# Moving matmul operands to other 64-byte quarters of a 256-byte line in a one-layer conformer and SwiGLU block

## The chip, the core and the metric

The kernel runs on one core of a Trainium2 chip. The metric is the device time of one execution in microseconds (us). TensorE multiplies (PE in the rows; PEld is its load of the stationary operand), VectorE is DVE, ScalarE is ACT, GpSimd is POOL, and SyncE (SP) issues the weight transfers. TensorE's granted clock was 1.00 of full speed, the 2.4 GHz level, in nearly the whole run.

## The reference, cut to what matters

One layer on 272 tokens (16 meta tokens and 256 real ones) with 2048 channels:

```
u = rms_norm(h, g1)
a, g = split(u @ w_in + b_in)               # 2048 x 4096
u = depthwise_conv31(a * sigmoid(g)) + b_dw
u = silu(layer_norm(u)) @ w_out + b_out     # 2048 x 2048
h = h + rms_norm(u, g2)
u = rms_norm(h, g3)
u = (silu(u @ w_gate) * (u @ w_up)) @ w_down  # 2048 x 5632 twice, 5632 x 2048
return (h + rms_norm(u, g4))[16:]
```

## The kernel before

**Split precision.** Every large product is made from fp32r operands in two parts: a high part (the value rounded) and a low part (the rest). ACT casts a raw fp32 weight block to its high part (L155), DVE or POOL subtracts to get the low part (L157). A product is high by high, high by low and low by high.

**Stages, in order.** "in" has 16 groups of two weight tiles; a step in depth is three matmuls of 272 columns (L218 to L220) with a weight part as the stationary operand and an activation part streaming: high weights by high activations, high weights by low activations, low weights by high activations. "out" and "gate/up" hold the high and low activations of a step side by side, so that a step is a pair: L227 streams 512 columns past the high weights, L228 streams 256 columns past the low weights (in the last out group, L223 does it in three matmuls of 256). There are 240 pairs in out and 1408 in gate/up, which has 22 groups of 4 weight tiles. "down" turns the roles round: 128 tokens of the SwiGLU result (tile `hid`) are stationary, and 512 columns of down weights stream past them, in threes (L773 to L775): high by high, high by low, low by high. There are 352 threes in down and 512 in in.

**Weight flow.** `PLAN` lists 360 blocks of at most 128 x 1024; `prep` fetches, casts and subtracts a block, up to three blocks ahead of TensorE. The order on PE, ACT, DVE and POOL is the order in which the code is written.

**Where operands start.** A partition's bytes can be counted in lines of 256 bytes (`LINE`, 64 values) and quarters of 64 bytes (16 values). In the built program every tile `hi`, `lo`, `hid` and `moving` begins at a multiple of 256. A weight tile of 128 columns is 512 bytes, so all tiles of a block begin at one quarter. The activations begin at quarter 0, but the low activations of in, which follow 272 columns of high ones, begin at quarter 1. The low weights of in, out and gate/up are put half a line in (`LO_AT` is 32 values), at quarter 2; all else begins at quarter 0.

The identity matrix `ident` (two POOL instructions) is made first of all; it is used for the convolution's diagonals and one matmul at the end of in.

Of the kernel before, what the change touches and what calls it, by code (L numbers as in the profile page):

```python
# [8 lines left out]
F32 = mybir.dt.float32  # L9
F32R = mybir.dt.float32r  # L10
# [3 lines left out]
P = 128  # L14
D = 2048
F = 5632
SEQ = 256
# [5 lines left out]
NF = F // P  # L23
RMS_EPS = 1e-6
LN_EPS = 1e-5
SB = 1024
# [15 lines left out]
def plan():  # L42
    out = []
    for name, groups, n_k in (
        ("in", IN_GROUPS, NK),
        ("out", OUT_GROUPS, NK),
        ("gu", FFN_GROUPS, NK),
        ("down", DOWN_GROUPS, NF),
    ):
        for g, tiles in enumerate(groups):  # L50
            n = len(tiles) * (2 if name == "gu" else 1)
            for k, kb in sub_blocks(n, n_k):
                out.append((name, g, n, k, kb))
    return out


PLAN = plan()
# [1 line left out]


LINE = 64
LO_AT = 32
MOVE = 2 * L + 32
LOOK = 3
RAW = 4

# [10 lines left out]
HID_LATE = 4  # L77
# [5 lines left out]
def conformer_swiglu_kernel(ctx: ExitStack, tc: tile.TileContext, xT, wflat, vec, w_dw, gain, out):  # L83
    nc = tc.nc
# [4 lines left out]
    const = ctx.enter_context(tc.tile_pool(name="const", bufs=1))  # L89
    wp = ctx.enter_context(tc.tile_pool(name="wp", bufs=4))  # L90
# [3 lines left out]
    def bank():  # L94
        return mm.tile([P, 512], F32, tag="bank", name="bank")
# [5 lines left out]
    def moving(cols, nm):  # L101

        t = xs.tile([P, NK, MOVE], F32R, tag="moving", name=nm)
        return t[:, :, :cols]
# [15 lines left out]
    last_sq = const.tile([P, SEQ], F32, name="last_sq")  # L120
    ones = const.tile([P, P], F32, name="ones")
    nc.gpsimd.memset(ones, 1.0 / D)
    ident = const.tile([P, P], F32, name="ident")
    make_identity(nc, ident)


    offs, off = [], 0
# [7 lines left out]
    def load(i):  # L135
        if i >= len(PLAN) or i in raws:
            return
        _, _, n, _, kb = PLAN[i]
        sz = n * kb * P
        raw = wp.tile([P, SB], F32, tag="raw", name="raw", bufs=RAW)  # L140
        nc.sync.dma_start(
            out=raw[:, :sz], in_=wflat[offs[i] : offs[i] + P * sz].rearrange("(p f) -> p f", p=P)
        )
        raws[i] = raw

    def prep(i):
        name, _, n, _, kb = PLAN[i]
        sz = n * kb * P
        for j in range(i, i + RAW):
            load(j)  # L150
        raw = raws.pop(i)
        hi = wp.tile([P, SB], F32R, tag="hi", name="hi")
        at = 0 if name == "down" else LO_AT
        lo = wp.tile([P, SB + LINE], F32R, tag="lo", name="lo")[:, at : at + SB]
        nc.scalar.copy(out=hi[:, :sz], in_=raw[:, :sz])  # L155
        eng = nc.gpsimd if i < FIRST["out"] + 10 or 0 <= i - FIRST["gu"] < 10 else nc.vector
        eng.tensor_tensor(  # L157
            out=lo[:, :sz], in0=raw[:, :sz], in1=hi[:, :sz].bitcast(F32), op=ALU.subtract
        )
        ready[i] = (hi, lo)  # L160

    def ahead(i, n):

        while n and state["next"] <= min(i + LOOK, len(PLAN) - 1) and state["next"] < state["cap"]:
            prep(state["next"])
            state["next"] += 1
            n -= 1

    def table(func):

        t = small.tile([P, 1], F32, tag="table", name="table")
        nc.scalar.activation(out=t, in_=ones[:, 0:1], func=func)
# [5 lines left out]
    def in_stages(tasks, start=0):  # L178
        for k, t in enumerate(tasks):
            for j, f in enumerate(t):  # L180
                while len(pending) <= start + k + j:
                    pending.append([])
                pending[start + k + j].append((-j, f))
# [6 lines left out]
    def matmuls(name, g, banks, moving, n_k, before=None, step=None, one_half=False, at={}):  # L190

        s_no = 0
        for i, (nm, gg, n, k0, kb) in enumerate(PLAN):
# [3 lines left out]
            if step and s_no:  # L197
                ahead(i, LOOK + 1)
            if step:
# [4 lines left out]
            else:  # L204
                ahead(i, LOOK + 1)
            hi, lo = ready.pop(i)
# [27 lines left out]
    def rsqrt(r, src, eps, n, between=None, first=None, fill=()):  # L234

        y = small.tile([P, L], F32, tag="rs_y", name="rs_y", bufs=1)
        nc.scalar.activation(out=y[:, :n], in_=src, func=AF.Abs_reciprocal_sqrt, bias=eps)  # L240
        m = small.tile([P, L], F32, tag="rs_m", name="rs_m", bufs=1)
        nc.scalar.mul(out=m[:, :n], in_=y[:, :n], mul=-0.5)
        if between:
            between()
        a = small.tile([P, L], F32, tag="rs_a", name="rs_a", bufs=1)
        nc.vector.tensor_tensor(out=a[:, :n], in0=y[:, :n], in1=y[:, :n], op=ALU.mult)
        if first:
            fy = last_sq
            nc.vector.scalar_tensor_tensor(
                out=fy[:, :n], in0=first[1], scalar=-0.5, in1=y[:, :n], op0=ALU.mult, op1=ALU.mult  # L250
            )
        nc.vector.scalar_tensor_tensor(out=a[:, :n], in0=src, scalar=eps, in1=a[:, :n], op0=ALU.add, op1=ALU.mult)
        for f in fill:
            f()
        if first:
            nc.vector.scalar_tensor_tensor(
                out=first[0], in0=a[:, :n], scalar=-3.0, in1=fy[:, :n], op0=ALU.add, op1=ALU.mult
            )
        nc.vector.scalar_tensor_tensor(out=r, in0=a[:, :n], scalar=-3.0, in1=m[:, :n], op0=ALU.add, op1=ALU.mult)
# [32 lines left out]
    xh, xl = x_mv[:, :, :L], x_mv[:, :, L:]  # L292
    front = tc.tile_pool(name="front", bufs=1)
    fr = front.__enter__()
    tp = ctx.enter_context(ExitStack())
    tmp = tp.enter_context(tc.tile_pool(name="tmp", bufs=2))
    done = {"x": 0, "ln": 0, "h": 0}
# [148 lines left out]
    def step(c, s, banks):  # L446
# [3 lines left out]
        if s == 0 and p >= 0:  # L450
            def behind_gate():
                ahead(4 * c, LOOK + 1)
                if c - 3 >= UNSHIFTED:
                    square(c - 3)
# [52 lines left out]
    b = conv(last, *glu_banks[last], lambda: None)  # L507
# [38 lines left out]
    def less_mean(c):  # L546
        lns[c] = zz[:, c, :SEQ]
        nc.vector.tensor_tensor(out=lns[c], in0=lns[c], in1=mean, op=ALU.subtract)

    def silu(c):  # L550
# [11 lines left out]
        rln, var, LN_EPS, SEQ, between=lambda: table(AF.Silu), first=(lns[0], lns[0]), fill=[lambda: less_mean(2)]  # L562
# [18 lines left out]
    acc = const.tile([P, SEQ], F32, name="acc")  # L581
# [27 lines left out]
    for g, tiles in enumerate(OUT_GROUPS):  # L609
        banks = [bank() for _ in tiles]  # L610
        end = g == len(OUT_GROUPS) - 1
        if end:
# [3 lines left out]
            at={NK - 5: drain, NK - 2: sum_of_squares} if end else {},  # L616
# [48 lines left out]


    r2 = const.tile([P, SEQ], F32, name="r2")
    acc2 = const.tile([P, SEQ], F32, name="acc2")
    cell = {}

    def add_squares(q):
# [7 lines left out]
    def factor():  # L679
        st = bank()  # L680
        nc.tensor.matmul(st[:, :SEQ], lhsT=ones, rhs=acc2, start=True, stop=True)
        rsqrt(r2, st[:, :SEQ], RMS_EPS, SEQ)

        sqs.__exit__(None, None, None)
        back = ctx.enter_context(tc.tile_pool(name="back1", bufs=1))
        cell["hids"].append(back.tile([P, HID_LATE, 2 * SEQ], F32R, name="hid1"))

    def hid(f, s):
        late = f >= NF - HID_LATE
        return cell["hids"][late][:, f - (NF - HID_LATE if late else 0), s]  # L690

    def swiglu(f, pg, pu):
        tb, ts = cell["tb"], []
# [25 lines left out]
    for g, tiles in enumerate(FFN_GROUPS):  # L719
        banks = [bank() for _ in range(4)]  # L720
        matmuls("gu", g, banks, h_mv, NK, before=residual if g == 0 else None)
        if g == 0:
            tp.close()
            front.__exit__(None, None, None)
            back = ctx.enter_context(tc.tile_pool(name="back0", bufs=1))
            cell["hids"] = [back.tile([P, NF - HID_LATE, 2 * SEQ], F32R, name="hid0")]
            cell["tb"] = ctx.enter_context(tc.tile_pool(name="tb", bufs=2))
            sqs = tc.tile_pool(name="sqs", bufs=2)
            cell["sqp"] = sqs.__enter__()
        tasks = [swiglu(f, banks[i], banks[2 + i]) for i, f in enumerate(tiles)]  # L730
        if g == 0:
            in_stages([[t[0]] for t in tasks])
            in_stages([[lambda q=q: add_squares(q)] for q in range(4)] + [[factor]])
            in_stages([t[1:] for t in tasks], start=5)
        else:
            in_stages([(lambda t=t: (t[0](), t[1]()), t[2], t[3]) for t in tasks])

    free = xs.tile([P, NK * MOVE], F32, tag="moving", name="free")
    tr = free[:, : NK * SEQ].rearrange("p (c t) -> p c t", c=NK)
# [102 lines left out]
    for g in range(len(DOWN_GROUPS)):  # L842
# [4 lines left out]
        late = mine[-LAG:] if g == len(DOWN_GROUPS) - 1 else []  # L847
        for i in mine:
            ahead(i, LOOK + 1)
            down(i, bs, (0,) if i in late else (0, 1))  # L850
# [67 lines left out]
```

## Time and profile before

| what | value |
|---|---|
| timed runs | 1063.78, 1067.93, 1068.65 us; median 1067.93 |
| profiled execution, its own time | 1064.57 us |
| its span, first to last instruction | 1062.8 us |
| PE busy, PEld busy | 99 %, 88 % of the span |
| granted TensorE clock, mean | 0.997 |

The span is what the rows below divide up; 1.8 us of the profiled execution's time lie around it. Busy time of PE says little, because a matmul's record runs on while the next one has begun (a record of 392 ns, a next start 229 ns later); the distance from start to start is what a matmul costs. The three timed runs lie 4.9 us apart.

### The profile page before, as it was taken

To read this page: it belongs to the slowest core of one execution; us is meant where nothing else is said; L and a number is where in the kernel's file an instruction comes from. 1 tells how busy PE (TensorE), PEld (TensorE's weight loads), DVE (VectorE), ACT (ScalarE), POOL (GpSimd) and SP (SyncE) were. 2 spreads that over 40 slices of the span, in tenths; PEclk is the share of its full clock that TensorE was granted. 3 is DMA by queue.
4 is the path that set the end of the run, shared out by engine and by line. 5 is a ranking of instruction groups with operands and counts; after the bars stand their busy time and mean duration, and the time that the engine had idled before them with its cause. 6 is when DMAs were issued, how large, how long until landed. Compare 5 with 4: busy or idle time off the path is not lost.

```text
span 1062.8 us, 16372 instructions
## 1 busy us (share of the span) xinstructions
PE 1048.7 (99%) x6142; PEld 932.2 (88%) x6142; DVE 692.4 (65%) x1193; ACT 584.3 (55%) x918; POOL 321.2 (30%) x191
## 2 busy tenths in 40 slices
PE   9999999999999999999999999999999999999996
PEld 8999999988888888888888888888888888888885
DVE  5699999987447866555666556665666635454544
ACT  6877877767567655444554445444454334343432
POOL 5889999955245111111111111111111000000000
PEclk9999999999999999999999999999999999999998
DMA  7555656527664666666666666666666896667662
GB/s 254 175 169 174 178 173 171 170 65 211 187 177 124 214 195 186 193 188 190 194 184 195 185 193 191 188 194 185 195 186 191 214 269 215 194 195 192 191 195 97
DMA packets 71841, 197.62 MB, mean 186 GB/s; under 512 B 22993, under 2 KB 24529, under 8 KB 71633
## 3 DMA queue, kind: packets, MB, share of 16 engines
q1 hardware_dynamic: 61728, 192.90, 61.6%
q10 hardware_dynamic: 10032, 3.67, 1.4%
q8 instruction: 48, 0.79, 0.3%
q14 instruction: 33, 0.26, 0.1%
HBM read 192.35 MB, written 2.10 MB: 183 GB/s over the span
## 4 chain that ended last, share of the span: by engine, by line
PE 96%; DVE 1%; DMA 1%; ACT 1%; issue 0%; SPq 0%; POOL 0%; DVEq 0%; ACTq 0%; POOLq 0%
PE bank L227 36%; PE bank L228 18%; PE bank L773 8%; PE bank L774 8%; PE bank L775 8%; PE bank L219 6%; PE bank L220 6%; PE bank L218 6%; DMA raw<-wflat 1%; PE bank L414 1%; PE bank L223 1%; ACT hi L155 0%; SPq L107 0%; POOL lo L157 0%; DVE x_mv L311 0%
## 5 line engine op out<-in xcount | busy, mean ns | idle before, releaser
L155 ACT CAST hi<-raw 128x1024 fp32r<-128x1024 f32 x360 | 377.8, 1050 | 418.1 <-PE bank L227 185.2
L157 DVE TENSOR_TENSOR lo<-raw,hi 128x1024 fp32r<-128x1024 f32 x276 | 341.1, 1236 | 315.7 <-ACT hi L155 315.6
L227 PE MATMUL bank<-h_mv,hi 128*128 128x512 f32 x1408 | 488.9, 392 | 1.2 <-DVE h_mv L645 1.2
L228 PE MATMUL bank<-h_mv,lo 128*128 128x256 f32 x1408 | 395.4, 281 | 0.0
L227 PEld LDWEIGHTS bank<-h_mv,hi 128*128 128x128 f32 x1408 | 264.3, 188 | 59.7 <-issue 1.3
L228 PEld LDWEIGHTS bank<-h_mv,lo 128*128 128x128 f32 x1408 | 264.7, 188 | 0.0
L157 POOL TENSOR_TENSOR lo<-raw,hi 128x1024 fp32r<-128x1024 f32 x84 | 201.2, 2405 | 49.4 <-ACT hi L155 47.9
L715 POOL TENSOR_TENSOR hid<-sw_s,hid 128x256 fp32r<-128x256 f32 x44 | 64.9, 1476 | 412.5 <-ACT hid L714 412.5
L218 PE MATMUL bank<-x_mv,hi 128*128 128x272 f32 x512 | 147.6, 288 | 0.8 <-ACT x_mv L310 0.4
L219 PE MATMUL bank<-x_mv,hi 128*128 128x272 f32 x512 | 147.9, 289 | 0.4
L220 PE MATMUL bank<-x_mv,lo 128*128 128x272 f32 x512 | 147.8, 289 | 0.0
L774 PE MATMUL bank<-lo,hid 128*128 128x512 f32 x352 | 136.9, 389 | 0.0
L773 PE MATMUL bank<-hi,hid 128*128 128x512 f32 x352 | 136.9, 389 | 0.0
L775 PE MATMUL bank<-hi,hid 128*128 128x512 f32 x352 | 136.9, 389 | 0.0
L390 DVE SCALAR_TENSOR_TENSOR bank<-u,taps,bank 128x256 f32<-128x256 f32 x293 | 129.8, 485 | 1.7 <-ACT bank L383 1.7
L218 PEld LDWEIGHTS bank<-x_mv,hi 128*128 128x128 f32 x512 | 96.3, 188 | 2.0 <-ACT sig L349 1.0
L219 PEld LDWEIGHTS bank<-x_mv,hi 128*128 128x128 f32 x512 | 96.2, 188 | 1.1 <-DVE x_mv L311 1.1
L220 PEld LDWEIGHTS bank<-x_mv,lo 128*128 128x128 f32 x512 | 96.2, 188 | 0.0
L227 PE MATMUL bank<-s_mv,hi 128*128 128x512 f32 x240 | 84.8, 397 | 0.9 <-DVE s_mv L574 0.9
L775 PEld LDWEIGHTS bank<-hi,hid 128*128 128x128 f32 x352 | 66.1, 188 | 13.8
L773 PEld LDWEIGHTS bank<-hi,hid 128*128 128x128 f32 x352 | 66.1, 188 | 13.7
L774 PEld LDWEIGHTS bank<-lo,hid 128*128 128x128 f32 x352 | 66.1, 188 | 13.6
(139 smaller groups left out, 824.8 us busy)
## 6 DMA issues: line engine op xcount, KB each, us to landing
raw<-wflat SPq DMA_DIRECT2D x360, 512.0 KB, 3.6
x_sb<-xT SPq DMA_DIRECT2D x3, 544.0 KB, 4.8
x_sb<-free SPq DMA_DIRECT2D x16, 64.0 KB, 4.6
x_sb<-free ACTq DMA_DIRECT2D x16, 64.0 KB, 5.5
free<-gain ACTq DMA_DIRECT2D x1, 1024.0 KB, 7.9
y<-free ACTq DMA_DIRECT2D x8, 128.0 KB, 2.4
y<-free ACTq DMA_DIRECT2D x2, 256.0 KB, 2.4
y<-free SPq DMA_DIRECT2D x2, 256.0 KB, 2.8
```

The source lines that it names most:

```text
L155: nc.scalar.copy(out=hi[:, :sz], in_=raw[:, :sz])
L157: eng.tensor_tensor(out=lo[:, :sz], in0=raw[:, :sz], in1=hi[:, :sz].bitcast(F32), op=ALU.subtract)
L218: nc.tensor.matmul(banks[t][:, :L], lhsT=hi[:, s], rhs=xh[:, kk, :], start=kk == 0, stop=False)
L219: nc.tensor.matmul(banks[t][:, :L], lhsT=hi[:, s], rhs=xl[:, kk, :], start=False, stop=False)
L220: nc.tensor.matmul(banks[t][:, :L], lhsT=lo[:, s], rhs=xh[:, kk, :], start=False, stop=kk == n_k - 1)
L227: nc.tensor.matmul(banks[t], lhsT=hi[:, s], rhs=moving[:, kk, :], start=kk == 0, stop=False)
L228: nc.tensor.matmul(banks[t][:, :SEQ], lhsT=lo[:, s], rhs=moving[:, kk, :SEQ], start=False, stop=kk == n_k - 1)
L390: nc.vector.scalar_tensor_tensor(out=t if j == nd - 1 else o, in0=u[:, j : j + SEQ], scalar=taps[:, c, j : j + 1], in1=o, op0=ALU.mult, op ...
L715: nc.gpsimd.tensor_tensor(out=hl, in0=ts[2], in1=hh.bitcast(F32), op=ALU.subtract)
L773: nc.tensor.matmul(bs[h], lhsT=xh, rhs=hi[:, s], start=f == 0, stop=False)
L774: nc.tensor.matmul(bs[h], lhsT=xh, rhs=lo[:, s], start=False, stop=False)
L775: nc.tensor.matmul(bs[h], lhsT=xl, rhs=hi[:, s], start=False, stop=f == NF - 1)
```

## The change

It changes where operands begin within a line, and nothing about which instructions there are.

- In out and gate/up the high weights begin at quarter 1 and the low ones at quarter 0 (before: 0 and 2).
- In in each of the 16 groups has its own pair: the high weights at quarter g // 4, the low ones at quarter g % 4 (before: 0 and 2 in every group).
- In down the four groups take the four pairs of quarters 0 and 1 for the high and low weights (before: 0 and 0).
- The 44 SwiGLU tiles stand in four sets of 11; the quarters of their high and low parts are (0, 0), (1, 0), (0, 1) and (1, 1) (before: 0 and 0).
- To make room, `ident` moves to the pool that ends with the front half, so that it is made later, and `acc2` shares the buffer of `acc`.

```diff
-LO_AT = 32
+QUARTER = 16
+def places(name, g):
+    if name == "in":
+        return g // 4 * QUARTER, g % 4 * QUARTER
+    if name == "down":
+        return g // 2 * QUARTER, g % 2 * QUARTER
+    return QUARTER, 0
+HID_BLOCK = F // P // 4
+HID_AT = [(0, 0), (1, 0), (0, 1), (1, 1)]
+def hid_places():
+    starts, col = {}, 0
+    for late in (False, True):
+        col = 0
+        for b, at in enumerate(HID_AT):
+            tiles = [f for f in range(b * HID_BLOCK, (b + 1) * HID_BLOCK) if (f >= F // P - HID_LATE) == late]
+            for w in range(2):
+                col += (at[w] * QUARTER - col) % LINE if tiles else 0
+                for f in tiles:
+                    starts[f, w] = col
+                    col += SEQ
+        starts[late] = col if late else (col + LINE - 1) // LINE * LINE
+    return starts
...
-    ident = const.tile([P, P], F32, name="ident")
-    make_identity(nc, ident)
...
-        hi = wp.tile([P, SB], F32R, tag="hi", name="hi")
-        at = 0 if name == "down" else LO_AT
-        lo = wp.tile([P, SB + LINE], F32R, tag="lo", name="lo")[:, at : at + SB]
+        hi_at, lo_at = places(name, g)
+        hi = wp.tile([P, SB + LINE], F32R, tag="hi", name="hi")[:, hi_at : hi_at + SB]
+        lo = wp.tile([P, SB + LINE], F32R, tag="lo", name="lo")[:, lo_at : lo_at + SB]
...
+    ident = fr.tile([P, P], F32, name="ident")
+    make_identity(nc, ident)
...
-    acc2 = const.tile([P, SEQ], F32, name="acc2")
+    acc2 = acc
...
-        late = f >= NF - HID_LATE
-        return cell["hids"][late][:, f - (NF - HID_LATE if late else 0), s]
+        c = hid_at[f, s.start // SEQ] + s.start % SEQ
+        return cell["hids"][f >= NF - HID_LATE][:, c : c + s.stop - s.start]
```

The built programs have the same rows on PE, DVE, ACT and SP, with the same waits. On POOL one thing moves. At the start of the program POOL's rows before were these, `ones` being the matrix of 1/2048 for the means, `lo` and `hi` the weight parts:

```order
L122 MEMSET ones 128x128
masks.py:197 MEMSET ident 128x128
masks.py:199 ISA
masks.py:199 AFFINE_SELECT ident<-ident 128x128
L157 TENSOR_TENSOR lo<-raw,hi 128x1024 x8
```

With the change, at the same place (L186 is the line that was L157):

```order
L153 MEMSET ones 128x128
L186 ISA
L186 TENSOR_TENSOR lo<-raw,hi 128x1024 x2
masks.py:197 MEMSET ident 128x128
masks.py:199 AFFINE_SELECT ident<-ident 128x128
L186 TENSOR_TENSOR lo<-raw,hi 128x1024 x6
```

The two instructions that make `ident` now stand behind the low parts of the first two weight blocks and ahead of the third.

## Rows read from the trace of the kernel before

**Rows 1.** The page's head: busy time by engine, granted clock in slices.
```profile
span 1062.8 us, 16372 instructions
...
PE 1048.7 (99%) x6142; PEld 932.2 (88%) x6142; DVE 692.4 (65%) x1193; ACT 584.3 (55%) x918; POOL 321.2 (30%) x191
...
PEclk9999999999999999999999999999999999999998
```

**Rows 2.** The chain that ended last, shares of the span by engine and line.
```profile
PE 96%; DVE 1%; DMA 1%; ACT 1%; issue 0%; SPq 0%; POOL 0%; DVEq 0%; ACTq 0%; POOLq 0%
PE bank L227 36%; PE bank L228 18%; PE bank L773 8%; PE bank L774 8%; PE bank L775 8%; PE bank L219 6%; PE bank L220 6%; PE bank L218 6%; DMA raw<-wflat 1%; PE bank L414 1%; PE bank L223 1%; ACT hi L155 0%; SPq L107 0%; POOL lo L157 0%; DVE x_mv L311 0%
```

**Rows 3.** Waits of PE: waited for, us in total, times, longest.
```profile
PE bank L227 <- DVE h_mv L645: 1.2, 1, 1.2
PE bank L266 <- POOL ones L122: 1.0, 1, 1.0
PE bank L227 <- DVE s_mv L574: 0.9, 1, 0.9
```

**Rows 4.** Line L227, gate/up, from 370 us: count, duration ns, first and last start.
```profile
L227 PE MATMUL bank<-h_mv,hi x1268: 392/392/392, 369.7 to 808.9; 128*128 128x512 f32 x182
```

**Rows 5.** Line L773 in down, the same columns.
```profile
L773 PE MATMUL bank<-hi,hid x331: 389/389/389, 820.2 to 1044.6; 128*128 128x512 f32 x166
```

**Rows 6.** Line L218 in in.
```profile
L218 PE MATMUL bank<-x_mv,hi x380: 285/287/288, 69.8 to 212.8; 128*128 128x272 f32 x190
```

**Rows 7.** Line L227 in out.
```profile
L227 PE MATMUL bank<-s_mv,hi x176: 392/394/475, 246.6 to 307.9; 128*128 128x512 f32 x176
```

**Rows 8.** Line L227, the first part of gate/up.
```profile
L227 PE MATMUL bank<-h_mv,hi x90: 392/394/395, 330.8 to 361.9; 128*128 128x512 f32 x90
```

**Rows 9.** Timeline of PE around 362 us: start, us, instruction.
```profile
361.94 0.39 PE L227 MATMUL bank<-h_mv,hi 128*128 128x512 f32 x1
362.17 0.28 PE L228 MATMUL bank<-h_mv,lo 128*128 128x256 f32 x1
362.29 0.59 PE L681 MATMUL bank<-acc,ones 128*128 128x256 f32 x2
362.53 0.58 PE L227 MATMUL bank<-h_mv,hi 128*128 128x512 f32 x1
362.95 0.28 PE L228 MATMUL bank<-h_mv,lo 128*128 128x256 f32 x1
```

**Rows 10.** Line L414, the convolution's fp32 matmuls, two records for each.
```profile
L414 PE MATMUL bank<-u,diags x38: 377/378/381, 213.2 to 221.2; 128*128 128x256 f32 x38
```

**Rows 11.** Groups by line, gate/up, 440 to 809 us: busy us, mean ns | idle before.
```profile
L228 PE MATMUL bank<-h_mv,lo 128*128 128x256 f32 x1065 | 299.3, 281 | 0.0
L228 PEld LDWEIGHTS bank<-h_mv,lo 128*128 128x128 f32 x1065 | 200.2, 188 | 0.0
...
L157 DVE TENSOR_TENSOR lo<-raw,hi 128x1024 fp32r<-128x1024 f32 x133 | 163.0, 1225 | 141.1 <-ACT hi L155 141.1
L155 ACT CAST hi<-raw 128x1024 fp32r<-128x1024 f32 x133 | 139.6, 1050 | 189.9 <-PE bank L227 131.5 <-issue 42.9 <-ACT sw_t L698 14.7
```

**Rows 12.** Groups by line, down, 815 to 1050 us.
```profile
L157 DVE TENSOR_TENSOR lo<-raw,hi 128x1024 fp32r<-128x1024 f32 x85 | 104.1, 1225 | 114.4 <-ACT hi L155 114.4
L155 ACT CAST hi<-raw 128x1024 fp32r<-128x1024 f32 x85 | 89.6, 1054 | 134.7 <-PE bank L775 114.3 <-DMA x_sb<-free 5.6 <-DMA raw<-wflat 5.4
```

**Rows 13.** The instructions of the tile ident: duration ns, first and last start.
```profile
masks.py:197 POOL MEMSET ident<- x1: 204/204/204, 0.9 to 0.9; 128x128 f32 x1
masks.py:199 POOL TENSOR_SCALAR_AFFINE_SELECT ident<-ident x1: 292/292/292, 1.2 to 1.2; 128x128 f32<-128x128 f32 x1
```

**Rows 14.** Line L157 on POOL up to 30 us.
```profile
L157 POOL TENSOR_TENSOR lo<-raw,hi x7: 2365/2390/2406, 13.8 to 28.2; 128x1024 fp32r<-128x1024 f32 x7
```

**Rows 15.** Timeline of PEld: the third block's first low tile is loaded.
```profile
23.42 0.19 PEld L220 LDWEIGHTS bank<-x_mv,lo 128*128 128x128 f32 x1
```

**Rows 16.** The chain in order of time: start us, us, what.
```profile
319.05 0.43 PE bank L606 x2
...
362.45 0.43 PE bank L681 x2
```

More of the change, by code (lines that the diff above doesn't have):

```diff
@@ L146, in prep @@
     def prep(i):
-        name, _, n, _, kb = PLAN[i]
+        name, g, n, _, kb = PLAN[i]
         sz = n * kb * P
@@ L685, in factor @@
         back = ctx.enter_context(tc.tile_pool(name="back1", bufs=1))
-        cell["hids"].append(back.tile([P, HID_LATE, 2 * SEQ], F32R, name="hid1"))
+        cell["hids"].append(back.tile([P, hid_at[True]], F32R, name="hid1"))
+    hid_at = hid_places()
     def hid(f, s):
-        late = f >= NF - HID_LATE
-        return cell["hids"][late][:, f - (NF - HID_LATE if late else 0), s]
+        c = hid_at[f, s.start // SEQ] + s.start % SEQ
+        return cell["hids"][f >= NF - HID_LATE][:, c : c + s.stop - s.start]
     def swiglu(f, pg, pu):
@@ L725, in conformer_swiglu_kernel @@
             back = ctx.enter_context(tc.tile_pool(name="back0", bufs=1))
-            cell["hids"] = [back.tile([P, NF - HID_LATE, 2 * SEQ], F32R, name="hid0")]
+            cell["hids"] = [back.tile([P, hid_at[False]], F32R, name="hid0")]
             cell["tb"] = ctx.enter_context(tc.tile_pool(name="tb", bufs=2))
```

## The prediction

> **What bounds the kernel now.** I read the page's head first: TensorE is busy for 99 % of the span, and its granted clock is 0.9 or more of full speed, the 2.4 GHz level, in nearly every slice [rows 1]. The chain that ended last agrees: 96 % of it is TensorE, and no other engine has over 1 % [rows 2]. The list of its waits is short, the longest 1.2 us [rows 3]. So only the distance from one matmul's start to the next can move the time, and I measured it by stage, from the first and last start of a line and its count:
>
> - gate/up, from 370 us on: (808.9 - 369.7) / 1267 = 346.6 ns for a pair [rows 4].
> - down: (1044.6 - 820.2) / 330 = 680.0 ns for three [rows 5].
> - in: (212.8 - 69.8) / 379 = 377.3 ns for three [rows 6].
> - out: (307.9 - 246.6) / 175 = 350.3 ns for a pair, and the first part of gate/up (361.9 - 330.8) / 89 = 349.4 [rows 7, 8].
>
> Down's three have 1536 columns and in's 816, so a column costs (680.0 - 377.3) / 720 = 0.42 ns, which is one column in a cycle of 2.4 GHz (0.4167). What is left above that is the stake of this change. Gate/up: 346.6 - 768 x 0.4167 = 26.6 for two matmuls, 13.3 each. Down: 680.0 - 640.0 = 40.0 for three, 13.3 each. In: 377.3 - 340.0 = 37.3, 12.4 each. Out: 350.3 - 320.0 = 30.3, 15.1 each. Over the kernel that is 1408 x 26.6 + 240 x 30.3 + 352 x 40.0 + 512 x 37.3 ns = 37.5 + 7.3 + 14.1 + 19.1 = 78 us.
>
> The reader should also see that the pair has **two states**. Out and gate/up have the same shapes and the same quarters, yet a pair takes about 350 in one and 346.6 in most of the other. The step comes where one small matmul (L681) breaks the row of pairs at 362.3 us [rows 9]: before it 349.4, after it 346.6. So the rhythm depends on how the row was entered. If the 1267 pairs behind it stayed in the slower state, the run would be 1267 x 3.3 = 4.2 us longer, an estimate that fits the timed runs: one at 1063.8, two at 1067.9 and 1068.7, while the profiled execution took 1064.6, of which 1062.8 is the span.
>
> **The change part by part.** While a matmul streams, the next one's stationary operand is loaded. I count the quarter of the load minus the quarter of the stream beside it.
>
> *Gate/up and out, before:* under L227 the low weights are loaded, distance 2; under L228 the next high weights, distance 0. *After:* 0 and 1. *What before shows of these:* down has distance 0 in all its loads and costs 13.3 each. Gate/up has 2 and 0 and costs 13.3 each. In has 0, 1 (low weights at quarter 2 beside low activations at quarter 1) and 0, and costs 12.4 each. So 0, 1 and 2 all stand in the trace, and they differ by at most 40.0 - 37.3 = 2.7 ns in three matmuls. I take **0** for 1648 pairs. The bounds: 16 columns, a quarter's worth, are 16 x 0.4167 = 6.7 ns, and one more or one fewer of these in a pair is 1648 x 6.7 = 11.0 us either way. I do not go further down, to the 2.9 ns that the convolution's fp32 matmuls show above their streaming time ((221.2 - 213.2) / 37 = 216.2 ns for 256 columns, which at half a column a cycle are 213.3 [rows 10]): those stream at half the rate, and no fp32r row is under 12.4.
>
> [...] The row shows that a loaded pair costs 13.3 ns a matmul above its columns [rows 4]. [...]
>
> *In:* each pair of quarters once over the 16 groups. The high loads meet distances 0 to 3 equally, the low loads too. With 0 to 2 seen as equal and 3 not seen: **0**, bounds as a quarter's worth for one load of three, 512 x 6.7 = 3.4 us either way.
>
> *Down:* streams and loads at quarter 0 or 1, so half of the 1056 loads at distance 0, a quarter at 1, a quarter at 3. **0**; bounds a quarter of the loads, 264 x 6.7 = 1.8 us either way.
>
> *Casts and subtractions* write 64 bytes further on. DVE's subtraction takes 1225 ns in gate/up, where it writes half a line in, and 1225 ns in down, where it writes at a line's start [rows 11, 12], so the start costs it nothing. ACT's cast is 1050 and 1054 there, and ACT waits mostly for TensorE to free a buffer, 131.5 us of its idle time in gate/up. Were a cast 10 % slower, 13 us over that stretch, it would lie in that idle time. **0.**
>
> *`ident`* is 0.204 + 0.292 = 0.50 us of POOL [rows 13], now ahead of the third low block. POOL makes low blocks back to back there at 2.39 us each from 13.8 us on [rows 14], so the third ends near 13.8 + 3 x 2.37 = 20.9 us, and with `ident` near 21.4. TensorE first loads from it at 23.42 us [rows 15]. The cover is 2 us: **0**; without it, 0.5 us once. POOL's queue behind it is 0.5 us late until its first idle moment. `acc2` in `acc`'s buffer is written only after L606 has read it at 319.05 us, and read by L681 at 362.45 [rows 16]; no wait arises. **0.**
>
> The sum is 0, so 1064.6 in the profiled execution's state, 1068.8 in the slower one.
>
> **The forecast and its rivals.**
>
> *The forecast: no visible effect.* For it: three distances cost the same. Against it: the two states show that a pair's rhythm can move by 3.3 ns with no change of work, so a new start can put it into a third. Time 1062.6 to 1073.3; within that 1063 to 1069.
> 1. *Distance 1 is the cheap one.* The 2.7 ns that in's three lack against down's would then all be its one load at distance 1. Gate/up and out get one such load in each pair: 1648 x 2.7 = -4.4 us. In has one of three now and 0.75 of three after: 512 x 0.25 x 2.7 = +0.3. Down gets 264: -0.7. Sum -4.8: 1059.8. If a pair loses a whole quarter's worth, -11.0: 1053.6. Against it: in differs from down in its columns too (272 instead of 512), which can explain the 2.7.
> 2. *The high load becomes too long for its cover* (slower). Under L228 only 256 columns stream, and the load beside it has no slack there: PEld's records of 188 ns follow each other through 88 % of the span [rows 1, 11]. A tile at quarter 1 touches three lines instead of two. If the third costs a quarter's worth, the pair is 6.7 longer: 1648 x 6.7 = +11.0, 1075.6; from 5.4 us, half of that, it decides the sign. Against it: in's low weights already touch three lines under 272 columns, and in has the smallest excess.
> 3. *The change does nothing to the stream but settles the state*: gate/up all in one state or the other, 1064.6 - 0.9 or 1068.8. It lies inside the forecast.
>
> **How the numbers follow.** What a measurement of this kernel can tell from no change is about 0.5 %, 5.3 us, so from the median 1067.9 "faster" begins under 1062.6 and "slower" above 1073.3. Chances: no visible effect 0.42 (rival 3 in it), rival 1 with its larger form 0.40, rival 2 and its half 0.18. The time of the likeliest is 1064, near the profiled state, since rows 4 show it holding for 1267 pairs once entered. For 8 in 10 the range takes in rival 1 up to most of its larger form, and rival 2 but for its full price: 1055 to 1074. The likeliest case's own range is 1063 to 1069.
>
> **What would show it.** Right: L256 and L257 (the lines that were L227 and L228) 346.6 or 350 ns from pair to pair, the same between groups of in with different quarters, PE's wait list as short as now. Rival 1: gate/up under 344.5, and in's groups differing by the quarters of `places`. Rival 2: pairs near 353, the gap behind L257 longer by 6 to 7. The forecast would be wrong if quarters mattered for the stream at all, most clearly if down's four groups or in's sixteen came out with different times for three.

## The result, and the profile after

The changed kernel is 0.6 % slower: 1073.23 us median (1071.15 to 1077.01, 5 runs) against 1067.54 (1063.78 to 1068.65, 5 runs), ratio 1.0064 with the interval 1.0045 to 1.0083. The forecast was 1064 and no visible effect. The profiled execution, the fastest of the five, took 1071.15 us, 6.6 more than that of before; its head answers to [rows 1]:

```profile
span 1069.3 us, 16373 instructions
...
PE 1055.2 (99%) x6142; PEld 934.1 (87%) x6142; DVE 692.8 (65%) x1193; ACT 583.6 (55%) x918; POOL 321.9 (30%) x191
```

TensorE is still the whole chain (shares of the span), and its longest wait is still 1.2 us (waited for, us in total, times, longest):

```profile
PE 96%; DVE 1%; DMA 1%; ACT 1%; issue 0%; SPq 0%; POOL 0%; DVEq 0%; ACTq 0%; POOLq 0%
```

```profile
PE bank L256 <- DVE h_mv L676: 1.2, 1, 1.2
```

So the distance from start to start has changed. First and last starts by line, the view of [rows 4 to 7]: L256 (was L227) in out and in gate/up, L806 (was L773) over all of down, and L247 (was L218) over all of in; under them the same two lines of before over all of down and in:

```profile
L256 PE MATMUL bank<-s_mv,hi x180: 389/389/401, 246.9 to 307.8; 128*128 128x512 f32 x180
L256 PE MATMUL bank<-h_mv,hi x1255: 393/393/396, 369.8 to 808.7; 128*128 128x512 f32 x180
L806 PE MATMUL bank<-hi,hid x352: 387/394/398, 816.7 to 1060.0; 128*128 128x512 f32 x176
L247 PE MATMUL bank<-x_mv,hi x512: 282/288/394, 16.2 to 212.4; 128*128 128x272 f32 x171
```

```profile
L773 PE MATMUL bank<-hi,hid x352: 389/389/395, 814.8 to 1053.5; 128*128 128x512 f32 x176
L218 PE MATMUL bank<-x_mv,hi x512: 285/287/396, 16.1 to 212.8; 128*128 128x272 f32 x171
```

| stage | before | after | what it makes |
|---|---|---|---|
| out, a pair | 350.3 ns | (307.8 - 246.9) / 179 = 340.2 | 180 x -10.1 = -1.8 us |
| gate/up, a pair | 346.6 | (808.7 - 369.8) / 1254 = 350.0 | 1267 x 3.4 = +4.3 us |
| down, a three | (1053.5 - 814.8) / 351 = 680.1 | (1060.0 - 816.7) / 351 = 693.2 | 243.3 - 238.7 = +4.6 us |
| in, first to last | 196.7 us | 196.2 us | -0.5 us |

That is +6.6 of the 6.5 us by which the spans differ. It compares two single executions; of the five timed runs of before four took 1067.30 to 1068.65 us, 3 to 4 more than its profiled one, and the experiments show where such a difference comes from. The strange part is the first two lines of the table: out and gate/up have the same shapes and, in the changed kernel, the same quarters, and they differ by 10 ns a pair. In the timeline of PE (start us, us, instruction), three matmuls of out and three of gate/up:

```profile
299.65 0.39 PE L256 MATMUL bank<-s_mv,hi 128*128 128x512 f32 x1
299.88 0.28 PE L257 MATMUL bank<-s_mv,lo 128*128 128x256 f32 x1
299.99 0.39 PE L256 MATMUL bank<-s_mv,hi 128*128 128x512 f32 x1
...
599.70 0.40 PE L256 MATMUL bank<-h_mv,hi 128*128 128x512 f32 x1
599.94 0.28 PE L257 MATMUL bank<-h_mv,lo 128*128 128x256 f32 x1
600.05 0.39 PE L256 MATMUL bank<-h_mv,hi 128*128 128x512 f32 x1
```

The identity matrix stands where the order said it would, at 18.6 us, and nothing waits for it:

```profile
masks.py:197 POOL MEMSET ident<- x1: 222/222/222, 18.6 to 18.6; 128x128 f32 x1
```

### The profile page after: what moved, and what is told of

Read it like the earlier page. It is cut to its first block, busy times and chain, and to the rows that moved or that the text cites. A ratio compares the mean times of both kernels' runs of the same rounds, so it can differ in the third digit from the quotient of the medians.

```text
span 1069.3 us, 16373 instructions
## 1 busy us (share of the span) xinstructions
PE 1055.2 (99%) x6142; PEld 934.1 (87%) x6142; DVE 692.8 (65%) x1193; ACT 583.6 (55%) x918; POOL 321.9 (30%) x191
## 4 chain that ended last, share of the span: by engine, by line
PE 96%; DVE 1%; DMA 1%; ACT 1%; issue 0%; SPq 0%; POOL 0%; DVEq 0%; ACTq 0%; POOLq 0%
PE bank L256 36%; PE bank L257 18%; PE bank L806 8%; PE bank L808 8%; PE bank L807 8%; PE bank L248 6%; PE bank L247 6%; PE bank L249 6%; DMA raw<-wflat 1%; PE bank L445 1%; PE bank L252 1%; ACT hi L184 0%; SPq L138 0%; POOL lo L186 0%; DVE free L863 0%
## 5 line engine op out<-in xcount | busy, mean ns | idle before, releaser
L184 ACT CAST hi<-raw 128x1024 fp32r<-128x1024 f32 x360 | 377.0, 1048 | 425.5 <-PE bank L256 191.0
L186 DVE TENSOR_TENSOR lo<-raw,hi 128x1024 fp32r<-128x1024 f32 x276 | 341.1, 1236 | 322.3 <-ACT hi L184 320.7
L256 PE MATMUL bank<-h_mv,hi 128*128 128x512 f32 x1408 | 493.2, 395 | 1.2 <-DVE h_mv L676 1.2
L256 PEld LDWEIGHTS bank<-h_mv,hi 128*128 128x128 f32 x1408 | 264.5, 188 | 60.9 <-issue 1.3
L186 POOL TENSOR_TENSOR lo<-raw,hi 128x1024 fp32r<-128x1024 f32 x84 | 202.2, 2420 | 48.0 <-ACT hi L184 44.8
L247 PE MATMUL bank<-x_mv,hi 128*128 128x272 f32 x512 | 148.0, 289 | 0.9 <-ACT x_mv L341 0.6
L808 PE MATMUL bank<-hi,hid 128*128 128x512 f32 x352 | 138.5, 393 | 0.0
L806 PE MATMUL bank<-hi,hid 128*128 128x512 f32 x352 | 138.5, 393 | 0.0
L247 PEld LDWEIGHTS bank<-x_mv,hi 128*128 128x128 f32 x512 | 96.3, 188 | 2.2 <-ACT x_mv L341 1.0
L256 PE MATMUL bank<-s_mv,hi 128*128 128x512 f32 x240 | 83.0, 393 | 0.9 <-DVE s_mv L605 0.9
L806 PEld LDWEIGHTS bank<-hi,hid 128*128 128x128 f32 x352 | 66.1, 188 | 15.1
```

The lines of the kernel that those rows point to most:

```text
L186: eng.tensor_tensor(out=lo[:, :sz], in0=raw[:, :sz], in1=hi[:, :sz].bitcast(F32), op=ALU.subtract)
L247: nc.tensor.matmul(banks[t][:, :L], lhsT=hi[:, s], rhs=xh[:, kk, :], start=kk == 0, stop=False)
L256: nc.tensor.matmul(banks[t], lhsT=hi[:, s], rhs=moving[:, kk, :], start=kk == 0, stop=False)
L806: nc.tensor.matmul(bs[h], lhsT=xh, rhs=hi[:, s], start=f == 0, stop=False)
L808: nc.tensor.matmul(bs[h], lhsT=xl, rhs=hi[:, s], start=False, stop=f == NF - 1)
```

## The experiments

The main theory, A: an arrangement of quarters has a few rhythms of its own into which load and stream lock, and the way in which a row of matmuls is entered picks one. Its rivals: the quarters are innocent and the moved tiles cost the time (B); a load has a fixed price by its distance to the stream (C); the two times belong to a run or stage, not to an entry (D); which rhythm follows an entry is chance (E).

**Four kernels that put parts back.** All are the changed kernel with other numbers in `places` and `HID_AT`; the edit shown is that of e1_back. e1_back has every quarter of before; e2_gu_out keeps the new ones in out and gate/up alone, e3_down in down alone, e4_in in in alone.

```diff
 def places(name, g):
     if name == "in":
-        return g // 4 * QUARTER, g % 4 * QUARTER
+        return 0, 2 * QUARTER
     if name == "down":
-        return g // 2 * QUARTER, g % 2 * QUARTER
+        return 0, 0
-    return QUARTER, 0
+    return 0, 2 * QUARTER
-HID_AT = [(0, 0), (1, 0), (0, 1), (1, 1)]
+HID_AT = [(0, 0)] * 4
```

e1_back: 

> The changed kernel with every operand back at the quarters of before; only the later identity, the shared buffer and the wider tiles stay. Theory A (each arrangement of quarters has its own few locked rhythms of load and stream, and the way a row of matmuls is entered picks one): 1064 to 1069 us, in at 377.3 ns for three, gate/up at 346.7 or 350 for a pair, down at 680. Theory B (the quarters are innocent, the moved identity and the layout of the pools cost the time): 1071 to 1077 us, as the changed kernel.

e2_gu_out: 

> Only out and gate/up have the new quarters (high 1, low 0); in and down have those of before. Theory A: out near 340 ns for a pair in most of its steady part, gate/up at 350 if it is entered as in the changed kernel, which is -2.4 and +4.4 us against the profiled run of before, so 1064 to 1069; near 1055 if gate/up should fall into the 340 rhythm. Theory C (a load has a fixed price by its distance to the stream, whatever the rhythm): out and gate/up have one and the same time for a pair.

e3_down: 

> Only down has the new quarters. Theory A: the 16 arrangements run at 680 to 700 ns for three as in the changed kernel, mean near 692, so 352 x 12 ns = +4.3 us on a run of 1064 to 1069, that is 1068 to 1073; the two arrangements in which all four parts share one quarter at 680. Theory C: arrangements with the same three distances have the same time.

e4_in: 

> Only in has the new quarters, a pair for each group. Theory A: groups between 370 and 380 ns for three as in the changed kernel, mean near 375.4 against 377.3, so about -1 us: 1063 to 1068. Theory C: groups with the same distances have the same time, and so group 2 (high 0, low 2), the arrangement of before, takes 377.3.

| kernel | median us (lowest to highest) | ratio to before, interval |
|---|---|---|
| before, in the same set | 1064.14 (1062.28 to 1071.57) | |
| e1_back | 1063.85 (1062.15 to 1068.59) | 0.9997 (0.9976 to 1.0018) |
| e2_gu_out | 1068.38 (1067.12 to 1069.62) | 1.0046 (1.0031 to 1.0061) |
| e3_down | 1068.31 (1066.92 to 1073.22) | 1.0052 (1.0031 to 1.0073) |
| e4_in | 1063.66 (1062.72 to 1068.30) | 0.9996 (0.9974 to 1.0018) |

B falls with e1_back: the later identity, the shared buffer and the wider tiles cost nothing that its ten runs show. New quarters in out and gate/up alone cost 4.2 us by the medians, and in down alone 4.2. Down's part is there in every trace with these quarters in down. Gate/up's part depends on the execution it is compared with, as e3_down shows: its gate/up (L256) has before's quarters, its down (L806) the new ones.

```profile
L256 PE MATMUL bank<-h_mv,hi x1256: 392/394/396, 369.8 to 809.0; 128*128 128x512 f32 x180
...
L806 PE MATMUL bank<-hi,hid x340: 387/395/399, 820.2 to 1055.4; 128*128 128x512 f32 x170
```

Gate/up runs at (809.0 - 369.8) / 1255 = 350.0 ns here, not at 346.6, and down at (1055.4 - 820.2) / 339 = 694; this execution took 1073.22 us, and the other four 1066.9 to 1069.6. So 350 is a time that before's quarters have too, and the 4 us of gate/up are a price only beside an execution of before that runs at 346.6. By the timed runs most do: of before's 20 in this set 14 took 1062.3 to 1064.9 us and 6 took 1068.1 to 1071.6. No execution of before from the upper cluster has a trace.

e2_gu_out has new quarters in out and before's in in. Out missed what was expected of it, and in moved with its quarters unchanged. Out (L256) ran at (307.9 - 249.8) / 166 = 350.0 ns, where the changed kernel had 340.2 with the same quarters; in (L247) ran at (210.6 - 84.8) / 337 = 373.3, where before had 377.3:

```profile
L256 PE MATMUL bank<-s_mv,hi x167: 392/396/397, 249.8 to 307.9; 128*128 128x512 f32 x167
...
L247 PE MATMUL bank<-x_mv,hi x338: 288/289/290, 84.8 to 210.6; 128*128 128x272 f32 x169
```

In e4_in (high 1, low 0) ran at (79.67 - 69.77) / 27 = 366.7 ns for three in its group, where the changed kernel had (79.85 - 69.76) / 27 = 373.7 (373.4 by the unrounded starts) in the same group. C, one fixed price for a distance, has no place for any of these. The stretch in e4_in, with its first and last start, and then the same in the changed kernel:

```profile
L247 PE MATMUL bank<-x_mv,hi x28: 285/285/286, 69.8 to 79.7; 128*128 128x272 f32 x28
...
69.77 0.28 PE L247 MATMUL bank<-x_mv,hi 128*128 128x272 f32 x1
...
79.67 0.29 PE L247 MATMUL bank<-x_mv,hi 128*128 128x272 f32 x1
```

```profile
L247 PE MATMUL bank<-x_mv,hi x28: 288/288/291, 69.8 to 79.8; 128*128 128x272 f32 x28
...
69.76 0.29 PE L247 MATMUL bank<-x_mv,hi 128*128 128x272 f32 x1
...
79.85 0.29 PE L247 MATMUL bank<-x_mv,hi 128*128 128x272 f32 x1
```

**New entries into the row of pairs.** e5_nudge_02 has before's quarters, e6_nudge_10 high 1 and low 0 in out and gate/up; both get an extra fp32 matmul that adds zeros, ahead of depth steps 4 and 10 of each group of gate/up from the third on (`zero` is a tile of zeros). These two, e7, e8 and e10 were timed once each (1076.51, 1074.28, 1077.01, 1073.18 and 1066.65 us), so their times decide nothing; what counts is the distances within one execution.

```diff
...
+        def nudge(i, g=g, banks=banks):
+            n = 140 + (2 * g + i) % 16
+            nc.tensor.matmul(banks[0][:, :n], lhsT=zero, rhs=last_sq[:, :n], start=False, stop=False)
...
+            at={4: lambda: nudge(0), 10: lambda: nudge(1)} if g > 1 else {},
```

e5_nudge_02: 

> All quarters of before (out and gate/up at 0 and 2), and in every group of gate/up from the third on two extra fp32 matmuls that add zeros, of 140 to 155 columns, ahead of depth steps 4 and 10: 40 new entries into the row of pairs. Theory A (the entry picks the rhythm): the stretches behind them come out at two or more fixed times for a pair, 346.7 and 350 among them, by the length of the extra matmul. Rival D (the two states are a matter of the run or of the stage, not of the entry): all stretches of one run at one time.

e6_nudge_10: 

> The same 40 entries with out and gate/up at quarters 1 and 0. Theory A: stretches at 350 and, since out reached it in the changed kernel, some at 340. Rival D: all at 350.

One such entry in e6's timeline, between the tail of a stretch at 350 ns and one at 340:

```profile
488.99 0.39 PE L258 MATMUL bank<-h_mv,hi 128*128 128x512 f32 x1
489.22 0.28 PE L259 MATMUL bank<-h_mv,lo 128*128 128x256 f32 x1
489.34 0.43 PE L758 MATMUL bank<-last_sq,zero 128*128 128x154 f32 x2
489.50 0.50 PE L258 MATMUL bank<-h_mv,hi 128*128 128x512 f32 x1
489.84 0.28 PE L259 MATMUL bank<-h_mv,lo 128*128 128x256 f32 x1
489.95 0.39 PE L258 MATMUL bank<-h_mv,hi 128*128 128x512 f32 x1
```

It costs 0.27 us: L259 follows its L258 by 0.34 us instead of the usual 0.23, and 0.16 lie ahead of that. Line L258 in four stretches one after the other, behind extra matmuls of 152, 153 and 154 columns:

```profile
L258 PE MATMUL bank<-h_mv,hi x24: 395/396/495, 466.5 to 474.7; 128*128 128x512 f32 x24
L258 PE MATMUL bank<-h_mv,hi x24: 393/394/495, 475.2 to 483.4; 128*128 128x512 f32 x24
L258 PE MATMUL bank<-h_mv,hi x16: 393/394/396, 483.7 to 489.0; 128*128 128x512 f32 x16
L258 PE MATMUL bank<-h_mv,hi x24: 389/389/500, 489.5 to 497.4; 128*128 128x512 f32 x24
```

They settle at 353.3, 350, 350 and 340 ns (median distance of starts in each). The group's start between the second and the third changes nothing; the extra matmuls do. Over the whole run e5's stretches take 346.7 or 350, nothing else, and e6's 340, 350 or 353.3. In e5 the 20 entries with an even number of columns led to 346.7, those with 141, 145 and 153 too, and those with 143, 147, 149, 151 and 155 to 350; each length gave the same each time that it came back. In e6 the same length behind the same rhythm always led to the same rhythm. D falls, and nothing here speaks for E.

**All pairs of quarters in gate/up.** e7_gu_map is e5 with `places` giving g % 16 // 4 and g % 4 in gate/up, and extra matmuls of 140 and 145 columns.

e7_gu_map: 

> Gate/up alone goes through the 16 pairs of quarters (high g // 4, low g % 4 for the first 16 groups, then again from 0 and 0), each with three entries: the group's start and two extra matmuls of 140 and 145 columns that add zeros. Theory A: times for a pair between 340 and 357 in steps of 1.67 ns or more, with (0, 2) at 346.7 or 350 and (1, 0) at 340 or 350. Theory C (a fixed price by distance): the three stretches of a group agree, and pairs whose low quarter and high quarter are the same distances from 0 are the only ones that count, with (0, 0) the cheapest or the dearest.

Worked out from the starts of L260 (median over a stretch of the mean of four neighbouring distances), ns for a pair; where the three stretches differ, all values:

| high at | low 0 | low 1 | low 2 | low 3 |
|---|---|---|---|---|
| 0 | 352.5 to 355 | 346.7 | 346.7, 350 | 346.7, 350 |
| 1 | 340, 350 | 353.3 | 350 | 353.3 |
| 2 | 352 | 346.7, 353.3 | 351.7 | 346.7, 353.3 |
| 3 | 340, 350 | 346.7, 353.3 | 346.7 | 354 |

Seven of the 16 pairs have stretches that differ, so C falls here too. The changed kernel's pair (1, 0) can be the best of all and can be worse than before's; two stretches of it, at its start and behind 140 columns:

```profile
L260 PE MATMUL bank<-h_mv,hi x16: 389/389/389, 415.8 to 420.9; 128*128 128x512 f32 x16
L260 PE MATMUL bank<-h_mv,hi x24: 393/394/486, 421.4 to 429.5; 128*128 128x512 f32 x24
```

(420.9 - 415.8) / 15 = 340, and 350 behind its first pair in the second (the starts shown are rounded to 0.1 us; the table goes by unrounded ones). In (0, 0) high and low weights begin at the quarter of the activations, and yet it is among the dearest, never under 352.5; its second group begins with (695.5 - 690.2) / 15 = 353:

```profile
L260 PE MATMUL bank<-h_mv,hi x16: 394/398/403, 690.2 to 695.5; 128*128 128x512 f32 x16
```

**The grain in down.** e8_down_fine has other starts in down, in values (16 are a quarter, 64 a line), and before's quarters elsewhere.

```diff
-        return g // 2 * QUARTER, g % 2 * QUARTER
+        return [(0, 0), (0, 32), (8, 8), (64, 0)][g]
-HID_AT = [(0, 0), (1, 0), (0, 1), (1, 1)]
+HID_AT = [(0, 0), (0, 2), (2, 2), (0.5, 0.5)]
```

e8_down_fine: 

> Only down is changed. Its four groups have the high and low weights at values 0 and 0, 0 and 32, 8 and 8, 64 and 0; the four sets of SwiGLU tiles have high and low at 0 and 0, 0 and 32, 32 and 32, 8 and 8 (64 values are a line of 256 bytes, 16 a quarter, 8 half a quarter). Theory A with a period of a line: 64 and 0 takes what 0 and 0 takes in every set; the cells in which all four starts agree take 680; the others 680 to 700. If the quarter is not the grain, the cells with 8 show times that no cell with whole quarters has. If only a line's start is good, all cells but the first and last group's first set are over 680.

Mean ns for three, from the starts of L806, from the third start of a cell on (rows: high and low weights; columns: high and low SwiGLU part):

| weights at | 0, 0 | 0, 32 | 32, 32 | 8, 8 |
|---|---|---|---|---|
| 0, 0 | 680.6 | 693.3 | 697.6 | 700.1 |
| 0, 32 | 686.7 | 693.9 | 686.6 | 700.0 |
| 8, 8 | 700.1 | 700.0 | 702.9 | 680.0 |
| 64, 0 | 680.0 | 693.3 | 697.6 | 700.1 |

A shift of the high weights by a whole line changes nothing: the first and last rows agree. The cells in which all starts agree take 680, at value 8 as well as at 0. So in down no start is good in itself; the starts must agree. (In gate/up that does not hold, by (0, 0) above.) The quarter is not the whole grain, since weights at 8 with SwiGLU parts at 0 take 700.1 and, in the changed kernel, weights at 16 with parts at 0 take 686.7. Four cells of the changed kernel, by L806: first (0, 0) with (0, 0), then (0, 0) with (1, 0), then (1, 0) with (1, 0) behind its first three, then (1, 1) with (0, 0), in quarters; below them e8's cell with all starts at value 8:

```profile
L806 PE MATMUL bank<-hi,hid x22: 389/389/396, 816.7 to 831.0; 128*128 128x512 f32 x22
L806 PE MATMUL bank<-hi,hid x22: 398/398/398, 831.7 to 846.4; 128*128 128x512 f32 x22
L806 PE MATMUL bank<-hi,hid x21: 390/397/398, 955.2 to 969.2; 128*128 128x512 f32 x21
L806 PE MATMUL bank<-hi,hid x22: 388/388/397, 1000.3 to 1014.7; 128*128 128x512 f32 x22
```

```profile
L806 PE MATMUL bank<-hi,hid x22: 389/389/395, 986.8 to 1001.1; 128*128 128x512 f32 x22
```

(831.0 - 816.7) / 21 = 681, (846.4 - 831.7) / 21 = 700, (969.2 - 955.2) / 20 = 700 and (1014.7 - 1000.3) / 21 = 686; at value 8 (1001.1 - 986.8) / 21 = 681. The first and the third cell have the same distances, 0 in all three loads, and are 20 ns apart, so C falls in down as well. The 16 cells take the same time, to 0.7 ns, in the changed kernel, in e3_down and in e12_after_entered, but no row of down was given another entry: whether down has several rhythms for one arrangement is open.

**One pair everywhere.** e9_one_pair has (1, 0) in in, out and gate/up, and 0 in down; nothing else is done.

e9_one_pair: 

> High weights at quarter 1 and low at 0 in in, out and gate/up, every down operand at quarter 0. Theory A: in at 373 or 366.7 ns for three (the two times that this pair has shown), out and gate/up at 340 or 350 by their entry, down at 680. So 1064.4 - 2.0 to -5.4 (in) - 0 to -2.4 (out) and +4.4 or -9.4 (gate/up): near 1065 if gate/up is entered into 350, near 1050 if into 340; the timed runs may split into these two. Theory C: one time, the same in all runs.

1068.57 us (1066.11 to 1071.47, 10 runs) beside 1068.11 of before in the same set, ratio 1.0015 (0.9997 to 1.0032): no gain. In is at (210.7 - 69.9) / 377 = 373.5, out near 353.7, gate/up at 350:

```profile
L247 PE MATMUL bank<-x_mv,hi x378: 288/288/288, 69.9 to 210.7; 128*128 128x272 f32 x189
...
L256 PE MATMUL bank<-s_mv,hi x109: 395/396/396, 269.6 to 307.8; 128*128 128x512 f32 x109
...
L256 PE MATMUL bank<-h_mv,hi x1255: 393/393/396, 369.9 to 808.8; 128*128 128x512 f32 x180
```

The hoped-for 1050 did not come, because a start is not enough without its entry.

**An entry of one's choice.** e10_nudge_two is e6 with extra matmuls of one length up to group 11 and of another behind it, `n = 146 if g < 12 else 150`.

e10_nudge_two: 

> Out and gate/up at quarters 1 and 0 and again two extra matmuls that add zeros in each group from the third on, but now of one length: 146 columns up to group 11, 150 from group 12. Theory A (the rhythm behind an entry follows from the rhythm before it and the length of the extra matmul alone): a stretch at 350 is followed by 340 after 146 columns, as it was before, and a stretch at 340 by 340 after 150; so the last ten groups stay at one time. Rival E (which rhythm follows is chance): 340, 350 and 353.3 mixed in both halves.

Once the first 146 columns had gone by in the third group, all stretches up to the end of the stage ran at 340.0. Ahead of it the row stood at 353.3; line L258 there and behind it:

```profile
L258 PE MATMUL bank<-h_mv,hi x21: 395/396/396, 362.8 to 369.9; 128*128 128x512 f32 x21
...
L258 PE MATMUL bank<-h_mv,hi x23: 389/389/390, 376.9 to 384.3; 128*128 128x512 f32 x23
```

With e6, where 146 columns led from 350 to 340, this length has led to 340 from each of the three rhythms.

**Two versions with four such entries.** Both get an extra matmul of 146 columns in out's second group and in gate/up's groups 0, 2 and 3 (group 2 because L712, which was L681, breaks the row in group 1). e12_after_entered is the changed kernel with nothing else; e11_best also has (3, 0) in in and 0 in all of down.

```diff
...
+    def enter(bank):
+        n = 146
+        return lambda: nc.tensor.matmul(bank[:, :n], lhsT=zero, rhs=last_sq[:, :n], start=False, stop=False)
...
+            at={0: {8: enter(banks[0])}, 2: {4: enter(banks[0])}, 3: {4: enter(banks[0])}}.get(g, {}),
```

e12_after_entered: 

> The changed kernel as it is, with the same four extra matmuls. Theory A: gate/up at 340 instead of 350, 1300 pairs x 10 ns = -13 us and +1.2 for the extra matmuls: 1058 to 1061 where the changed kernel took 1071 to 1077, and so faster than before with the quarters unaltered. If the 350 belongs to the quarters of gate/up and not to the entry: 1072 to 1078.

e11_best: 

> In at quarters 3 and 0, out and gate/up at 1 and 0, all of down at 0, and four extra matmuls of 146 columns that add zeros: one in out's second group, three in gate/up (groups 0, 2 and 3). Theory A: in near 370 ns for three, out (from its second group) and gate/up (from its first) at 340 in every run, down at 680. Against the faster kind of run of before, 1064.4: in -3.7, out -2.2, gate/up -8 to -9.5, extra matmuls +1.2, so 1049 to 1052, and no two kinds of timed runs any more. Rival E (which rhythm follows is chance): timed runs spread from 1050 to 1066.

e12_after_entered took 1058.79 us (1058.63 to 1058.98, 5 runs), ratio 0.9930 (0.9905 to 0.9955); e11_best 1051.32 us (1051.05 to 1051.56, 5 runs), ratio 0.9858 (0.9835 to 0.9881), with before at 1064.44. Line L262 of e11_best ahead of L712, between L712 and the extra matmul of group 2, behind that matmul, and from group 4 on; then in's L253, and L262 of e12_after_entered:

```profile
L262 PE MATMUL bank<-h_mv,hi x63: 388/389/390, 335.6 to 356.7; 128*128 128x512 f32 x63
...
L262 PE MATMUL bank<-h_mv,hi x39: 393/394/397, 357.8 to 371.1; 128*128 128x512 f32 x39
...
L262 PE MATMUL bank<-h_mv,hi x47: 388/389/390, 372.1 to 387.7; 128*128 128x512 f32 x47
...
L262 PE MATMUL bank<-h_mv,hi x1133: 388/389/390, 414.9 to 799.7; 128*128 128x512 f32 x189
...
L253 PE MATMUL bank<-x_mv,hi x373: 282/287/288, 70.0 to 207.6; 128*128 128x272 f32 x187
```

```profile
L262 PE MATMUL bank<-h_mv,hi x1134: 388/389/390, 414.7 to 800.0; 128*128 128x512 f32 x189
```

(371.1 - 357.8) / 38 = 350.0, then (387.7 - 372.1) / 46 = 339 (340.0 by the unrounded starts) and (799.7 - 414.9) / 1132 = 339.9; in is at 369.9; e12's gate/up is at (800.0 - 414.7) / 1133 = 340.1. So the changed quarters of gate/up, which took 4 us more than before's profiled execution, take 8 us less than it when the row is entered rightly, the extra matmuls included, and the spread of the timed runs shrinks to 0.5 us. Ahead of L712 the row stood at (356.7 - 335.6) / 62 = 340.3; the 350 behind it shows that the rhythm was lost there until the next extra matmul.

## Why the prediction was wrong

- *What bounds the kernel* was right: the distances of TensorE's starts make +6.6 of the 6.5 us.
- *The step that failed* is "So 0, 1 and 2 all stand in the trace, and they differ by at most 40.0 - 37.3 = 2.7 ns in three matmuls. I take **0** for 1648 pairs." It took the price of a load from its distance to the stream beside it, one load at a time, and carried it from one arrangement to another. The runs showed that the price goes by the whole arrangement, and in in, out and gate/up by the rhythm that the row was entered into as well: (1, 0) has 340, 350 and 353.3 for a pair, before's (0, 2) has 346.7 and 350. In down three loads at distance 0 take 680 in one cell and 700 in another. The 2.7 ns themselves were an estimate that rests on the third digit of a column's time: the rows give 302.7 / 720 = 0.4204 ns, 2.38 columns in a ns, and with this in place of 0.4167 down and in have the same excess, 34.3 ns, as they must where the column is worked out from these two.
- *Down's term* was mis-sized by the same step: forecast 0 with 1.8 us to either side, measured +4.6. Its bound priced a quarter of the loads; 14 of the 16 cells are slower than before's 680, by 7 to 23 ns for three. The prediction had named down's groups coming out at different times as the clearest sign of being wrong.
- *Out and gate/up*, forecast 0, measured -1.8 and +4.3 beside before's profiled execution. But 350 is a rhythm of before's quarters too, and the forecast had priced its slower state at 4.2 us: gate/up alone would not have shown the step to be wrong, out at 340.2 and down do.
- *In* was forecast at 0 with 3.4 to either side; -0.5 was measured, since cheap pairs (370 at (3, 0)) and dear ones (380 at (0, 3)) cancel.
- *The two states* of before were read rightly from one step in the trace [rows 9]. The estimate that they explain the timed runs (4.2 us) agrees with the two clusters of before's 20 runs, and with e3_down's trace: 1064.57 + 4.0 for gate/up + 4.6 for down (both from first to last start, beside before's trace) = 1073.2 of the measured 1073.22. The prediction also named the danger, that "a new start can put it into a third", but gave it no price.
- The measured median lies inside the stated 1055 to 1074. That is luck: the upper part of the range stood for rival 2, and what filled it was down and the slower rhythm of gate/up.
- *Rival 1* (distance 1 cheap) had the size right for what (1, 0) can do, a loss of one quarter's worth a pair, 346.7 - 340.0 = 6.7, but only with the right entry; in down the cell with two of its three loads at distance 1, (0, 0) with (1, 0), is among the dearest, 700, so distance 1 is not cheap in itself. *Rival 2* (the high load too long for its cover) is not needed: the same quarters run at 340 in out.
- `ident` and `acc2` cost nothing that the runs show, as forecast: e1_back's ratio is 0.9997 (0.9976 to 1.0018). With their new starts the casts took 377.0 us of ACT against 377.8, and the subtractions 341.1 of DVE against 341.1 and 202.2 of POOL against 201.2.
- That the changed kernel's timed runs reach 1077 is not settled: gate/up at 353.3 instead of 350 would give 1267 x 3.3 = 4.2 us of these 5.9, and out at 350, as in e2_gu_out, 1.8, but only one of its executions has a trace.
- What in the chip makes these rhythms stays open. That the time depends on where load and stream begin relative to each other is measured: 693.2 against 680.1 ns for three in down, and in e8_down_fine 680.0 with all starts at value 8, 680.6 with all at 0, 700.1 with the weights alone at 8. That a load and the stream beside it wait for each other is a reading, and no run separates it from another cause of the same steps.

## What to carry to other kernels

When TensorE is the whole chain, measure the distance of starts for each stage and look for steps in it where nothing in the work changes: two values there can mean a rhythm that can be chosen. Do not look for one good start: in down the starts did best when all agreed (680.0 ns for three), in gate/up that was among the worst (352.5 to 355 for a pair). Try the pairs in one run, a group each, with several entries for each, since a single entry can show a pair's worse rhythm. A short matmul that adds zeros was a cheap way (0.27 us) to choose the rhythm of a row of a thousand pairs; its length had to be found by trial, and it has to follow whatever breaks the row.

## What the runs showed of the hardware

- Start to start, an fp32r pair of 512 and 256 columns took 340.0, 346.7, 350.0 or 353.3 ns at mean granted clocks of 0.998 and 0.997 in 12 of the 16 pairs of quarters (e7_gu_map; for (1, 0) also e6_nudge_10), up to three of these for one arrangement with the same work; the steps between neighbours are 6.7 and 3.3 ns, the time of 16 or 8 columns at the 0.42 ns that [rows 5, 6] give for one. The other four pairs of quarters took 351.7 to 355.
- In in, before's quarters took 377.3 or 373.3 ns for three (before, e2_gu_out), and (1, 0) took 373.4 or 366.7 (the changed kernel, e4_in).
- Where operands begin within 256 bytes moves three matmuls of 512 columns in down between 680.0 and 703 ns. A shift of all operands by 32 bytes (680.0 in e8_down_fine) or 64 (680.0 in the changed kernel), or of the high weights by 256 (680.0 beside 680.6 in e8_down_fine), moves nothing there.
- A column cost 0.42 ns in fp32r ((680.0 - 377.3) / 720, [rows 5, 6]) and 0.84 in the convolution's fp32 records (216.2 / 256, [rows 10]), at a granted clock of 1.00 in these stretches.
- The rhythm behind an extra matmul was the same each time the same length followed the same rhythm, over 40 entries in each of three executions (e5, e6, e10), and five timed runs each of e11 and e12 lay within 0.5 us.
